# The first 100 microseconds of a decoder layer: zero matmuls ahead of the loads, another order of loads and weights, masks and token shift written later

## The chip, the cores and the metric

The kernel runs on one core of one Trainium2 chip. The metric is the device time of one execution in microseconds; the time before is the median of three executions. A profile is one further execution that the hardware profiler recorded, with a span (first to last instruction) and a time of its own.

## The reference

One hybrid decoder layer over 1024 tokens of width 1024, all in float32:

```python
u = rmsnorm(h, norm1_g)
proj = u @ w_in
p_rwkv, p_att, p_idx, p_gate = jnp.split(proj, c, axis=-1)
y_a = rwkv7_mix(token_shift(p_rwkv, tshift_mu), ...)      # recurrent mixing, 8 heads
q_idx = rope(q_idx.reshape(B, S, IDX_HEADS, IDX_DIM))     # indexer: 8 query heads, one key head
k_idx = rope(k_idx[:, :, None, :])[:, :, 0, :]
y_b = dsa_attention(q, k, v, q_idx, k_idx, w_idx)         # attention over the indexer's top 256 keys
merged = g_a * (y_a @ w_o_rwkv) + g_b * (y_b @ w_o_att)
h = h + merged @ w_out
z_gate, z_up = jnp.split(rmsnorm(h, norm2_g) @ w_ffn_in, 2, axis=-1)
h = h + (jax.nn.silu(z_gate) * z_up) @ w_ffn_out
return rmsnorm(h, normf_g)

def token_shift(p, mu):
    prev = jnp.pad(p, ((0, 0), (1, 0), (0, 0)))[:, :-1]
    return p + (prev - p) * mu
```

## The kernel before

**Arithmetic.** Activations lie with features on the partitions and tokens along the free dimension, in two halves of 512 tokens. To keep float32 accuracy with the fast float32r matmul, every operand is split into a high and a low part (`whi`/`wlo` for weights, `u0hi`/`u0lo` for the first half of x, `u1hi`/`u1lo` for the second). ScalarE makes the high part, VectorE subtracts for the low one, and `mm3` adds up high x high, high x low and low x high: per half 24 matmuls for one 128-column tile of weights and eight tiles of 128 features.

**Opening.** `first` loads two weight tiles (CT_IK, the indexer's key and weights, and CT_WA, the decay and rate columns) and sixteen tiles of x through SP's DMA queue, splits them, and runs both weight tiles over both halves. x is not normalized first: `Rms` sums the squares beside the matmuls (`add`), `columns` and `row` make the reciprocal root, and every result is scaled by it afterwards (`scale`, `rows[half]`).

**Next stage.** `proj_iq` projects the indexer's queries (CT_IQ, CT_IQ + 1), then runs `rest` and the generator `between`, and then projects CT_IQ + 2 and CT_IQ + 3. `rest` applies the token shift (`shifted`, lines 281 to 287) to the CT_WA result, stores it to `d_rw`, rotates the indexer's key (`rope_one`) and stores it to `d_ik`. `between` is the projection of CT_GD with its own token shift. After it come the tiles of k (the first ones before the scores), and `scores` loads `ik` and, for each block of 128 queries, `iq` from DRAM and runs the score matmuls (line 860) with pieces of the remaining projections between them (`pump`).

**What sets the order.** TensorE's instructions stand in the order in which the source writes them:

```python
ctx.enter_context(tc.manual_schedule(engines={mybir.EngineType.PE}))
```

For VectorE, ScalarE, SP's DMA queue and GpSimd a scheduler chooses the order when the kernel is built; each engine and queue then runs its list strictly in order, and waits at the first instruction whose input is not there. Buffers rotate: three accumulators of one PSUM bank each (`acc`), five further banks (`mix`), four temporaries (`tmp`), two staging buffers (`stg`, from which results are stored to DRAM), two pairs of split weights, three raw weight tiles (`wst`). A tile that takes a buffer waits for the last reader of the tile before it; for `stg` that reader is a store.

**Masks.** `masks` loads the causal mask (`caus`) and fills the bias of the first two query blocks at line 836; these biases are read in the attention stage, hundreds of microseconds later.

Of the kernel before, what the change touches and what calls it, by code (L numbers as in the profile page):

```python
# [11 lines left out]
F32 = mybir.dt.float32  # L12
# [37 lines left out]
def block_kernel(ctx: ExitStack, tc: tile.TileContext, ins: dict, outT: bass.AP, stop=None, dbg=None):  # L50
# [54 lines left out]
    def mix():  # L105
        return psM.tile([128, HT], F32, tag="mix", name="mix")
# [10 lines left out]
    def raw_weights(src, nk=8):  # L117
        st = wp.tile([128, nk, 128], F32, tag="wst", name="wst", bufs=3)
        wq[0].dma_start(st, src)
        return st  # L120

    def weights(src, nk=8, rush=True, st=None, pool=None):
        with tc.high_priority() if rush else nullcontext():
            if st is None:
                st = raw_weights(src, nk)
            hi, lo = ((pool or wp).tile([128, nk, 128], F32R, tag=tag, name=tag, bufs=8 if pool else None)
                      for tag in ("whi", "wlo"))
            split(hi, lo, st)
        return hi, lo
# [121 lines left out]
    def gsplit(hi, lo, x, gcol):  # L251

        g = par[:, gcol:gcol + 1]
        A.activation(hi, x, AF.Copy, scale=g)
        V.scalar_tensor_tensor(lo, x, g, hi.bitcast(F32), op0=ALU.mult, op1=ALU.subtract)

    def load_x(half, h, js):
        src = ins["xT"][:, half * HT:(half + 1) * HT].rearrange("(k p) t -> p k t", p=128)
        for j in js:
            SY.dma_start(h[:, j, :], src[:, j, :])  # L260
# [80 lines left out]
    def first(us, xp, pj, cp2, cs):  # L341

        hs = [xp[half].tile([128, 8, HT], F32, tag=f"h{half}", name="h") for half in range(2)]
        st0 = raw_weights(ins["w_in"][CT_IK])
        load_x(0, hs[0], range(2))
        st1 = raw_weights(ins["w_in"][CT_WA])
        load_x(0, hs[0], range(2, 8))
        load_x(1, hs[1], range(8))
        SY.dma_start(cs, ins["rope"])
        ws = [weights(None, st=st, rush=False) for st in (st0, st1)]  # L350
        sqs, raws = [], []
        for half, h in enumerate(hs):
            for k in range(8):
                gsplit(us[half][0][:, k, :], us[half][1][:, k, :], h[:, k, :], P_N1 + k)
            sqs.append(Rms(h))
            for k in range(8):
                sqs[half].add(k)
            uhi, ulo = us[half]
            pss = [acc(), acc()]
            for k in range(8):  # L360
                for (whi, _), ps in zip(ws, pss):
                    T.matmul(ps, whi[:, k, :], uhi[:, k, :], start=k == 0, stop=False)
                    T.matmul(ps, whi[:, k, :], ulo[:, k, :], start=False, stop=False)
            for (_, wlo), ps in zip(ws, pss):
                for k in range(8):
                    T.matmul(ps, wlo[:, k, :], uhi[:, k, :], start=False, stop=k == 7)
            raw = cp2.tile([128, HT], F32, tag=f"raw{half}", name="raw")
            A.activation(raw, pss[0], AF.Copy)
            wa = cp2.tile([128, HT], F32, tag=f"wa{half}", name="wa")
            A.activation(wa, pss[1], AF.Copy)  # L370
            raws.append((raw, wa))
        def scale(half):
            rows[half] = sqs[half].row()
            for i in range(2):
                c = cs[:, i, half * HT:(half + 1) * HT]
                V.tensor_tensor(c, c, rows[half], op=ALU.mult)

        def rest():
            st = stage(pj)
            for half in range(2):  # L380
                shifted(st, half, CT_WA, raws[half][1])
            SY.dma_start(d_rw[CT_WA][0], st.rearrange("p h t -> p (h t)"))
            for half in range(2):
                ik = rope_one(cs, raws[half][0], half)
                kst = stage(pj, F32R)
                split(kst[0:64, 0, :], kst[0:64, 1, :], ik[0:64, :])
                for i in range(2):
                    SY.dma_start(d_ik[half].rearrange("c (p s) t -> s p c t", s=2)[i],
                                 kst[32 * i:32 * i + 32, :, :].bitcast(F32))

        return sqs, scale, rest, raws

    def proj_iq(us, pj, cs, between, sqs, scale, rest, raws):
        off = 256
        sqs[0].columns(rsk[:, 0, :])
        wa = weights(ins["w_in"][CT_IQ], rush=False)
        psa = [mix(), mix()]
        yield from mm3(psa[0][:, :HT - off], wa, us[0], tok=slice(off, HT))
        sqs[1].columns(rsk[:, 1, :])
        yield from mm3(psa[1], wa, us[1])  # L400
        wb = weights(ins["w_in"][CT_IQ + 1])
        for half, o in enumerate((off, 0)):
            ps = acc()
            yield from mm3(ps[:, :HT - o], wb, us[half], tok=slice(o, HT))
            scale(half)
            rope_b(cs, ps, rope_a(cs, psa[half], half, o), pj, [(slice(0, 128), d_iq[half][:, 0:4])], half, o)
        rest()
        yield from between
        yield from proj_rope(CT_IQ + 2, us, pj, cs, lambda half: [(slice(0, 128), d_iq[half][:, 4:8])], off=off)
        for half in range(2):  # L410
            pt = mix()
            for t in range(4):
                T.transpose(pt[:, t * 128:(t + 1) * 128], raws[half][0][:, t * 128:(t + 1) * 128], ident)
            for t in range(4):
                V.tensor_scalar(widx[:, 4 * half + t, :], pt[:, t * 128 + 64:t * 128 + 72], rsk[:, half, t:t + 1],
                                64 ** -0.5 * 8 ** -0.5, op0=ALU.mult, op1=ALU.mult)
            yield 4
# [404 lines left out]
    def masks(bp, p):  # L822

        caus = p.tile([128, 128], F32, name="caus")
        G.dma_start(caus, ins["consts"][:, K_CAUS, :])
        bias, kept = {}, {}
        for b in range(8):
            n = (b + 1) * 128
            if b in LATE:
                kept[b] = bp.tile([128, n], F32, name=f"kept{b}")  # L830
                bias[b] = kept[b].bitcast(BF16)[:, 0:n]
            else:
                bias[b] = bp.tile([128, n], BF16, name=f"bias{b}")
            if b < 2:
                V.memset(bias[b], 0.0)
                V.tensor_scalar(bias[b][:, b * 128:], caus, BIG / 3.0e38, None, op0=ALU.mult)
        bp.tile([128, 16], F32, name="edge")
        return caus, bias, kept

    def scores(keep, p, caus, kept):  # L840

        ik = p.tile([128, 2, S], F32R, name="ik")
        for h in range(2):
            for e in range(2):
                SY.dma_start(ik[64 * e:64 * e + 64, :, h * HT:(h + 1) * HT].bitcast(F32),
                             d_ik[h].rearrange("c p t -> p c t"))
        sc = {}
        for b in range(2, 8):
            n = (b + 1) * 128
            iq = p.tile([128, 8, 128], F32R, tag="iq", name="iq", bufs=2)  # L850
            o = (b % 4) * 128
            for i in range(2):
                SY.dma_start(iq[64 * i:64 * i + 64, :, :].bitcast(F32),
                             d_iq[b // 4][i, :, :, o:o + 128].rearrange("h p t -> p h t"))
            s = kept[b] if b in kept else keep.tile([128, n], F32, tag=f"sc{b}", name="sc")
            for c, w in pieces(n):
                for h in range(8):
                    ps = mix()
                    for i in range(2):
                        T.matmul(ps[:, :w], iq[:, h, :], ik[:, i, c:c + w], start=i == 0, stop=i == 1)  # L860
                    rl = p.tile([128, 512], F32, tag="rl", name="rl", bufs=3)
                    A.activation(rl[:, :w], ps[:, :w], AF.Relu)
                    if h == 0:
                        V.tensor_scalar(s[:, c:c + w], rl[:, :w], widx[:, b, 0:1], 0.0, op0=ALU.mult, op1=ALU.add)
                    else:
                        V.scalar_tensor_tensor(s[:, c:c + w], rl[:, :w], widx[:, b, h:h + 1], s[:, c:c + w],
                                               op0=ALU.mult, op1=ALU.add)
                    pump(2)
            V.tensor_tensor(s[:, n - 128:n], s[:, n - 128:n], caus, op=ALU.add)
            sc[b] = s  # L870
        return sc
# [544 lines left out]
```

## Time and profile before

| | |
|---|---|
| median of three executions | 1773.98 us (1772.75 to 1774.41) |
| profiled execution, its own time | 1776.56 us |
| its span | 1774.8 us |
| mean granted TensorE clock | 0.993 |
| TensorE busy | 1731.5 us |
| VectorE busy | 1117.6 us |
| ScalarE busy | 832.2 us |

In the lines of the profile, PE is TensorE's matmuls, PEld its weight loads, DVE VectorE, ACT ScalarE, POOL GpSimd, and SPq the DMA queue that SyncE issues. A line of a timeline has the start, the time taken, the engine, the line of the source, the operation, the tile written and the tiles read, the shapes and how many instructions were merged; in brackets stands how long the engine had been idle and what ended the idling. A line of waits has who waited for whom, the sum in microseconds, how often, and the longest. Matmuls are pipelined, so the time of one is longer than the step from its start to the next one's.

### The profile page before, as it was taken

The numbers are of one execution on the slowest core, as the hardware profiler recorded it, in microseconds if no ns is written. First come the engines' busy times: TensorE is split into PE (matmuls) and PEld (weight loads), VectorE is DVE, ScalarE is ACT, GpSimd is POOL, SyncE is SP. The second block draws the span as 40 slices with busy tenths as digits, with TensorE's granted clock in tenths as the row PEclk, the third lists the DMA queues.
The fourth block names the chain that finished last, engine by engine and source line by source line (L and its number), as shares of the span: only waits on it lengthen the run. The fifth ranks groups of instructions, "written<-read, shape, count | busy, mean of one in ns | idle before, by whom it ended". The sixth has DMA issues, their size and how long they took to land. (4 is left out here: it accounts for less than half of the span.)

```text
span 1774.8 us, 26838 instructions
## 1 busy us (share of the span) xinstructions
PE 1731.5 (98%) x10256; PEld 1432.1 (81%) x10256; DVE 1117.6 (63%) x2137; ACT 832.2 (47%) x1535; POOL 93.5 (5%) x120
## 2 busy tenths in 40 slices
PE   7999999999999999999999999999999999999997
PEld 6888888788888777777888888888788888888877
DVE  5779989866468568847865655524565564454464
ACT  6355998453444788654233455523334322232231
POOL 0000000010021110001000311000000000000000
PEclk9999999999999999999999999999999999999999
DMA  5542224536375535723244854243565344434441
GB/s 207 165 138 90 101 95 143 164 86 176 92 203 171 148 108 173 227 88 110 78 119 113 240 154 119 76 139 112 185 206 154 108 135 148 143 97 156 129 139 64
DMA packets 130992, 244.00 MB, mean 137 GB/s; under 512 B 36536, under 2 KB 59704, under 8 KB 130736
## 3 DMA queue, kind: packets, MB, share of 16 engines
q1 hardware_dynamic: 107472, 168.38, 30.7%
q10 hardware_dynamic: 15552, 47.75, 8.8%
q0 software_dynamic: 7840, 26.15, 5.6%
q8 instruction: 81, 1.33, 0.3%
q14 instruction: 47, 0.39, 0.1%
HBM read 189.29 MB, written 52.95 MB: 136 GB/s over the span
## 5 line engine op out<-in xcount | busy, mean ns | idle before, releaser
L113 DVE TENSOR_TENSOR wlo<-wst,whi 128x1024 fp32r<-128x1024 f32 (+1 forms) x231 | 277.8, 1204 | 306.1 <-PE acc L143 139.7
L112 ACT ACTIVATE whi<-wst 128x1024 fp32r<-128x1024 f32 (+1 forms) x231 | 240.6, 1043 | 282.3 <-PE acc L139 224.0
L138 PE MATMUL acc<-zhi,whi 128*128 128x512 f32 x672 | 265.8, 396 | 1.3 <-DVE tmp L1189 1.3
L139 PE MATMUL acc<-zlo,whi 128*128 128x512 f32 x672 | 262.8, 391 | 0.0
L143 PE MATMUL acc<-zhi,wlo 128*128 128x512 f32 x672 | 170.1, 392 | 0.0
L138 PEld LDWEIGHTS acc<-zhi,whi 128*128 128x128 f32 x672 | 126.8, 189 | 28.5 <-issue 3.4
L138 PE MATMUL acc<-fhi,whi 128*128 128x512 f32 (+1 forms) x400 | 145.0, 371 | 3.9 <-ACT fhi L112 3.9
L139 PEld LDWEIGHTS acc<-zlo,whi 128*128 128x128 f32 x672 | 126.8, 189 | 25.0
L143 PEld LDWEIGHTS acc<-zhi,wlo 128*128 128x128 f32 x672 | 124.8, 188 | 25.5 <-issue 0.7
L139 PE MATMUL acc<-flo,whi 128*128 128x512 f32 (+1 forms) x400 | 143.7, 367 | 1.4 <-DVE flo L113 1.2
L138 PE MATMUL acc<-u1hi,whi 128*128 128x512 f32 x352 | 140.5, 399 | 0.1
L138 PE MATMUL acc<-u0hi,whi 128*128 128x512 f32 (+1 forms) x352 | 135.3, 387 | 4.2 <-DVE tmp L281 2.4
L139 PE MATMUL acc<-u1lo,whi 128*128 128x512 f32 x352 | 137.6, 391 | 0.0
L139 PE MATMUL acc<-u0lo,whi 128*128 128x512 f32 (+1 forms) x352 | 133.7, 382 | 0.0
L143 PE MATMUL acc<-fhi,wlo 128*128 128x512 f32 (+1 forms) x400 | 92.6, 369 | 0.0
L138 PEld LDWEIGHTS acc<-fhi,whi 128*128 128x128 f32 x400 | 76.1, 190 | 17.9 <-ACT fhi L112 5.8
L143 PE MATMUL acc<-u1hi,wlo 128*128 128x512 f32 x352 | 89.7, 394 | 0.0
L139 PEld LDWEIGHTS acc<-flo,whi 128*128 128x128 f32 x400 | 76.2, 190 | 14.6 <-DVE flo L113 3.3
L143 PE MATMUL acc<-u0hi,wlo 128*128 128x512 f32 (+1 forms) x352 | 86.0, 384 | 0.0
L112 ACT ACTIVATE fhi<-tmp 128x512 fp32r<-128x512 f32 x44 | 27.8, 631 | 113.7 <-DVE tmp L1169 113.7
L138 PEld LDWEIGHTS acc<-u0hi,whi 128*128 128x128 f32 x352 | 66.1, 188 | 17.5 <-issue 2.6
L143 PEld LDWEIGHTS acc<-fhi,wlo 128*128 128x128 f32 x400 | 69.6, 191 | 12.1 <-issue 0.5
(304 smaller groups left out, 3146.0 us busy)
## 6 DMA issues: line engine op xcount, KB each, us to landing
wst<-in_w_ffn_in SPq DMA_DIRECT2D x72, 512.0 KB, 3.7
wst<-in_w_in ACTq DMA_DIRECT2D x36, 512.0 KB, 3.7
wst<-in_w_in SPq DMA_DIRECT2D x27, 512.0 KB, 3.7
wst<-in_w_fo SPq DMA_DIRECT2D x25, 512.0 KB, 3.7
k<-d_k POOLq DMA_DIRECT2D x24, 512.0 KB, 8.3
h<-in_xT SPq DMA_DIRECT2D x32, 256.0 KB, 5.2
d_g<-tmp ACTq DMA_DIRECT2D x32, 256.0 KB, 3.0
tmp<-d_g SPq DMA_DIRECT2D x32, 256.0 KB, 3.1
```

The lines of the kernel that those rows point to most:

```text
L112: A.activation(hi, x, AF.Copy)
L113: V.tensor_tensor(lo, x, hi.bitcast(F32), op=ALU.subtract)
L138: T.matmul(ps, whi[:, wk + k, :], ahi[:, ak + k, tok], start=k == 0, stop=False)
L139: T.matmul(ps, whi[:, wk + k, :], alo[:, ak + k, tok], start=False, stop=False)
L143: T.matmul(ps, wlo[:, wk + k, :], ahi[:, ak + k, tok], start=False, stop=k == nk - 1)
```

## The change

Four edits, all of the first stage.

- Six float32 matmuls over the zeroed state tile are written ahead of everything else on TensorE; nothing reads their results.
- The loads of x come three tiles, then the second weight tile, then the rest (before: two, weight, rest). The weights' high parts are written where the loads arrive, their low parts after all eight low parts of the first half of x. On TensorE the first weight tile runs three feature tiles ahead of the second.
- In `proj_iq` the projection of CT_GD (`between`) comes before `rest`.
- The multiplies that fill the first two biases move from `masks` to the start of `scores`.

```diff
     def first(us, xp, pj, cp2, cs):
         hs = [xp[half].tile([128, 8, HT], F32, tag=f"h{half}", name="h") for half in range(2)]
+        for _ in range(6):
+            T.matmul(mix()[:, 0:256], state[:, 0:2, :].rearrange("p c t -> p (c t)"),
+                     state.rearrange("p c t -> p (c t)"), start=True, stop=True)
+        lead = 3
         st0 = raw_weights(ins["w_in"][CT_IK])
-        load_x(0, hs[0], range(2))
+        load_x(0, hs[0], range(lead))
         st1 = raw_weights(ins["w_in"][CT_WA])
-        load_x(0, hs[0], range(2, 8))
+        load_x(0, hs[0], range(lead, 8))
         load_x(1, hs[1], range(8))
         SY.dma_start(cs, ins["rope"])
-        ws = [weights(None, st=st, rush=False) for st in (st0, st1)]
+        ws = [tuple(wp.tile([128, 8, 128], F32R, tag=tag, name=tag) for tag in ("whi", "wlo")) for _ in range(2)]
         sqs, raws = [], []
         for half, h in enumerate(hs):
+            if half == 0:
+                A.activation(ws[0][0], st0, AF.Copy)
             for k in range(8):
+                if half == 0 and k == lead:
+                    A.activation(ws[1][0], st1, AF.Copy)
                 gsplit(us[half][0][:, k, :], us[half][1][:, k, :], h[:, k, :], P_N1 + k)
+            if half == 0:
+                for (whi, wlo), st in zip(ws, (st0, st1)):
+                    V.tensor_tensor(wlo, st, whi.bitcast(F32), op=ALU.subtract)
             ...
-            for k in range(8):
-                for (whi, _), ps in zip(ws, pss):
-                    T.matmul(ps, whi[:, k, :], uhi[:, k, :], start=k == 0, stop=False)
-                    T.matmul(ps, whi[:, k, :], ulo[:, k, :], start=False, stop=False)
+            for i in range(8 + lead):
+                for (whi, _), ps, k in zip(ws, pss, (i, i - lead)):
+                    if 0 <= k < 8:
+                        T.matmul(ps, whi[:, k, :], uhi[:, k, :], start=k == 0, stop=False)
+                        T.matmul(ps, whi[:, k, :], ulo[:, k, :], start=False, stop=False)
     ...
     def proj_iq(us, pj, cs, between, sqs, scale, rest, raws):
+        yield from between
         rest()
-        yield from between
     ...
     def masks(bp, p):
                 V.memset(bias[b], 0.0)
-                V.tensor_scalar(bias[b][:, b * 128:], caus, BIG / 3.0e38, None, op0=ALU.mult)
     ...
     def scores(keep, p, caus, kept):
+        for b in range(2):
+            V.tensor_scalar(bias[b][:, b * 128:], caus, BIG / 3.0e38, None, op0=ALU.mult)
         ik = p.tile([128, 2, S], F32R, name="ik")
```

## The prediction

> **What bounds the kernel now.** I read the page first, then the waits of TensorE, then the timeline of the first 100 us engine by engine, because the change touches nothing later.
>
> ```profile
> span 1774.8 us, 26838 instructions
> ...
> PE 1731.5 (98%) x10256; PEld 1432.1 (81%) x10256; DVE 1117.6 (63%) x2137; ACT 832.2 (47%) x1535; POOL 93.5 (5%) x120
> ```
>
> TensorE is busy for 98% of the span, and its instructions stand in a fixed order. A delay that TensorE gets early therefore stays until the end, and a wait that goes is a gain, unless another wait opens behind it. The answer on TensorE's waits in the first 200 us has three rows:
>
> ```profile
> PE acc L362 <- ACT u0hi L254: 6.7, 1, 6.7
> PE acc L363 <- DVE u0lo L255: 2.7, 1, 2.7
> PE acc L138 <- DVE tmp L281: 2.4, 1, 2.4
> ```
>
> Two belong to the opening (nothing loaded, then no low part of x), and the third is an accumulator that VectorE had not emptied. These 11.8 us are all that the change can win by waits. Because the rest is one queue of matmuls, I walk the changed kernel's built instruction order with the durations below until TensorE meets its first wait-free stretch; in that order 13 instructions of ScalarE, 26 of VectorE and 9 of SP's queue stand elsewhere than before, all of them in the first 110 us.
>
> **Opening: masks and low parts.** The timeline of VectorE:
>
> ```profile
> 8.00 0.36 DVE L836 TENSOR_SCALAR bias<-caus 128x128 bf16<-128x128 f32 x2 [2.86 <-DMA caus<-in_consts]
> 8.28 1.22 DVE L113 TENSOR_TENSOR wlo<-wst,whi 128x1024 fp32r<-128x1024 f32 x1
> 9.42 1.41 DVE L255 SCALAR_TENSOR_TENSOR u0lo<-h,par,u0hi 128x512 fp32r<-128x512 f32 x2
> 10.74 1.22 DVE L113 TENSOR_TENSOR wlo<-wst,whi 128x1024 fp32r<-128x1024 f32 x1
> ```
>
> The first low part of x ends near 10.1, behind the two mask multiplies (which wait for their load until 8.00) and a weight's low part of 1.22. The source of the changed kernel writes the multiplies and the weights' low parts later, but a scheduler orders VectorE, and the built order still has both mask multiplies first, then the first `wlo`, then three `u0lo` (two before), the second `wlo`, and the other five. So the first low part is as late as before, and these edits bring nothing: that part of the change doesn't do what it says. The fourth low part now ends near 13.3: 9.42 + 3 x 0.67 = 11.4, the `wlo` to 12.6, one more `u0lo`. The second weight's load moves back by one x tile of 0.26 MB, 0.65 us at the 401 GB/s that the first window further down shows; its low part ran at 10.74 before and is wanted at 11.4 now, so nothing waits.
>
> **Opening: matmuls on zeros.** The timeline of TensorE:
>
> ```profile
> 6.72 0.79 PE L362 MATMUL acc<-u0hi,whi 128*128 128x512 f32 x1 [6.72 <-ACT u0hi L254]
> 10.22 0.79 PE L363 MATMUL acc<-u0lo,whi 128*128 128x512 f32 x1 [2.70 <-DVE u0lo L255]
> ...
> 13.79 0.63 PE L363 MATMUL acc<-u0lo,whi 128*128 128x512 f32 x1
> 14.22 0.52 PE L362 MATMUL acc<-u0hi,whi 128*128 128x512 f32 x1
> 14.58 0.40 PE L363 MATMUL acc<-u0lo,whi 128*128 128x512 f32 x1
> 14.81 0.39 PE L362 MATMUL acc<-u0hi,whi 128*128 128x512 f32 x1
> ```
>
> and, from the same view much later, the nearest float32 matmul of this size:
>
> ```profile
> 381.83 1.89 PE L622 MATMUL mix<-x,blk 128*128 128x256 f32 x8
> ```
>
> Until 14.5 a matmul starts every 0.43 us, then every 0.23: the clock is half at first (the page prints 1.00 there for want of a record). The change issues six float32 matmuls of 256 columns once the state tile is cleared, near 1.4. L622 has eight records, two to a matmul, in 1.89 (the last one's 0.38 overlaps the next line's work), so about 0.45 each at full clock and 0.9 at half: 5.4 us, to 6.8. They cost nothing themselves, because TensorE has nothing else until 6.72 and the next matmul needs the low part at 10.2; the PSUM buffers that they write are not wanted before the second half of x is through. After them TensorE has one matmul and then 3 us of idling. Does the clock survive that? The windows before and after two clock records:
>
> ```profile
> 11.08:14.49 3.41, 3.41 (x9) 2.64 (x9) 3.41 (x5) 3.41 (x7) 0.00 (x0) 1.00 1.05 401
> 843.93:847.30 3.37, 3.18 (x14) 2.96 (x15) 2.89 (x7) 0.24 (x1) 0.00 (x0) 0.50 0.55 158
> 847.30:850.76 3.46, 3.46 (x11) 2.78 (x10) 3.46 (x6) 2.13 (x4) 0.00 (x0) 0.50 0.02 5
> 1277.40:1280.84 3.44, 1.92 (x7) 0.86 (x5) 2.22 (x5) 2.77 (x5) 0.00 (x0) 1.00 0.80 291
> 1280.84:1284.25 3.41, 3.38 (x8) 2.71 (x9) 1.17 (x2) 1.06 (x1) 0.00 (x0) 0.50 0.54 156
> ```
>
> Columns: length, busy time of TensorE, weight loads, VectorE, ScalarE and GpSimd, then the granted clock. A window in which TensorE was busy for 1.92 of 3.44 is followed by one at half clock; a window busy for 3.18 of 3.37 did not bring the full clock back; one busy throughout (11.08 to 14.49) did. Three idle microseconds cannot be cut by a window's edge so that both sides keep more than 56%. So I take the clock as half again at 10.2. Then the new order of the first weight ahead of the second hurts: before the fourth low part (13.3) it offers only seven matmuls, the last at 12.52, so TensorE idles for about 0.4 and is one matmul behind at 14.5 (10 issued, not 11): +0.2. If the idle moment also denies that window the full clock, as 3.18 of 3.37 was denied, the next 3.4 us hold 8 matmuls instead of 15: +1.8 in all. I take +1.8, nearest to that row; the ends are +0.2 and, with the clock full from 10.2, 41 matmuls of 0.227 from 13.3 to 22.6, against 37 from 14.58 to 23.0: -0.4.
>
> [...]
>
> **Token shift later.** VectorE's timeline, then TensorE's:
>
> ```profile
> 65.32 1.22 DVE L113 TENSOR_TENSOR wlo<-wst,whi 128x1024 fp32r<-128x1024 f32 x1 [1.07 <-PE acc L143]
> ...
> 69.72 0.68 DVE L281 TENSOR_TENSOR tmp<-acc,row 128x512 f32<-128x512 f32 x1
> ```
>
> ```profile
> 66.98 1.12 PE L143 MATMUL acc<-u0hi,wlo 128*128 128x256 f32 x8
> 70.55 0.35 PE L138 MATMUL acc<-u0hi,whi 128*128 128x256 f32 x1 [2.45 <-DVE tmp L281]
> ```
>
> In the new order the first accumulator of the tile CT_GD is read at 59.8, ahead of the token shift: the 2.45 us go. What is late next: the shift, the halo and the key rotation, which filled VectorE's idling before 65.32, now stand behind that `wlo` and ahead of the two reads that free the next accumulator. From 65.32: `wlo` 1.15, four shifts of 0.67, three products and seven rotation steps of 0.6, two half reads of 0.34, small ones 0.35: 10.9, to 76.2. TensorE asks for it after 24 matmuls of 0.12 and 24 of 0.227 from 67.9, at 76.3. That is level. One step, at 74.6, needs a ScalarE copy of 0.6 into a staging buffer whose store to DRAM goes out at 69.7; with the 3.3 to 5.9 us of landing shown below that copy ends at 73.6 to 76.2, so the wait is 0 to 1.6, and I take 0.3, since a store that lands in 4.6 adds 0.3.
>
> **What it puts into SP's queue.** This is the expensive part. SP's queue, the landing time of the `iq` loads, the first score matmul, and VectorE around it:
>
> ```profile
> 87.00 0.57 SPq L853 DMA_DIRECT2D iq<-d_iq  x1
> 89.16 0.98 SPq L315 DMA_DIRECT2D d_iq<-stg  x2
> 90.18 2.88 SPq L853 DMA_DIRECT2D iq<-d_iq  x3
> 97.72 0.35 SPq L119 DMA_DIRECT2D wst<-in_w_in  x1
> 100.05 0.34 SPq L294 DMA_DIRECT2D d_rw<-stg  x1
> ```
>
> ```profile
> DMA to landing us min/median/max: 3.3/5.2/5.9
> ```
>
> ```profile
> 99.83 0.51 PE L860 MATMUL mix<-ik,iq 128*128 128x384 f32 x2
> ```
>
> ```profile
> 96.47 1.23 DVE L113 TENSOR_TENSOR wlo<-wst,whi 128x1024 fp32r<-128x1024 f32 x1 [1.73 <-PE acc L143]
> 97.61 0.68 DVE L281 TENSOR_TENSOR tmp<-acc,row 128x512 f32<-128x512 f32 x1
> 99.09 0.75 DVE L283 SCALAR_TENSOR_TENSOR stg<-tmp,par,stg 128x511 f32<-128x511 f32 x1 [0.79 <-ACT stg L282]
> 99.76 0.21 DVE L287 SCALAR_TENSOR_TENSOR stg<-halo,par,stg 128x1 f32<-128x1 f32 x1
> ```
>
> The first score matmul (L860, 99.83) needs both halves of the first `iq` tile; before, they are issued at 87.00 and 90.18. In the changed order SP's queue holds, one behind the other: the `d_ik` stores, two weights that wait for VectorE's `wlo`, the `d_iq` stores and `ik` loads, one more weight (the one of 97.72), the first half of `iq`, the store `d_rw` of the first k tile (the one of 100.05), and only then the second half of `iq`. SP waits in order, so this half cannot be issued before that store, which hangs on the chain of 96.47 to 99.76 behind TensorE's own last matmul of that tile. The store comes at 100.05 less what TensorE has gained by then; the load is issued 0.38 later, and lands 3.3 to 5.9 later (all loads of this tile between 60 and 130 us). TensorE stands at the first score matmul, which it would reach 0.22 before the store: a wait of L + 0.6, with L the landing. I take L = 4.6, the middle, since two 512 KB transfers go just ahead: a wait of 5.2.
>
> Such a wait costs more than itself: at least one window is mostly idle, so the matmuls behind it run at half clock for one window (3.4 us, loss 1.7, as at 1280.84) or two (3.4, as from 843.93). I take 1.7.
>
> **Sum.** Gain before the scores: 2.45 - 0.3 - 1.8 = 0.35. Then 0.6 + 4.6 - 0.35 = 4.85 late at the first score, and 1.7 for the clock: +6.5. The profiled execution took 1776.56 (1774.8 of span and 1.8 around it), so 1783.1 by its own measure; carried to the median of 1773.98, 1780.5. Ends: +3.4 (opening +0.2, no wait after the shift, L 3.3, one half window) to +10.9 (+1.8, 1.6, 5.9, two windows): 1777.4 to 1784.9. Two high tiles of the second half that ScalarE now makes before it empties an accumulator are at nothing, since TensorE reads them after 23. Behind the first score matmul the built order is the old one, and TensorE has no wait there before 200 us in which the delay could vanish.
>
> **Rivals.**
> 1. The load is in time, and the kernel is faster. The second half of `iq` would have to land before TensorE's arrival near 97 to 99, so be issued before about 94. Then only the gain stays: -0.4 (0.35) to -2.9 (opening -0.4, no wait), and about -4.5 if unprofiled runs pay a half window after the old 2.45 us wait. For it: before, the loads landed with over 2 us to spare. Against: the store ahead in the queue, whose data does not exist by then. Chance 0.12; 1770 to 1773.6, likeliest 1772.
> 2. The clock stays full through both gaps: opening -0.4, a gain of 2.85, then 0.6 + L - 2.85 with L 3.3 to 4.6 and no half window: +1.1 to +2.4, 1775 to 1776.4. For it: the dummies do keep TensorE busy for 5.4 us, more than a window. Against: the row at 1277.40. Chance 0.14. [...]
> 3. Later than my upper end: the wait after the shift takes 1.6, the load 5.9 and the clock more than two windows; above 1784.9. Chance 0.04.
>
> **How the numbers follow.** The forecast has 0.70 and its own range of 1777.4 to 1784.9. Rival 2 and most of the forecast are held by 1775.5 to 1784.5, with rival 1 and the tail left out. A measurement of this kernel can tell 0.2%, 3.5 us, from no change. Faster by more needs the far end of rival 1: 0.04. Within it lie rival 2, the rest of rival 1 and the low edge of the forecast: 0.14 + 0.08 + 0.03 = 0.25. Slower by more: 0.71.
>
> **What would show it.** Right: both mask multiplies still ahead of the first `wlo` at about 8 us; a TensorE wait of some 0.4 on the fourth `u0lo`; no wait on L281 near 70; the `iq` load behind the `d_rw` store at about 100; one wait of 4 to 6.5 us on the first score matmul, released by a DMA, and a half-clock record behind it. Wrong: matmuls 0.23 apart from 10.2 on, or a first score matmul before 99.8.

## Result and the profile after

The changed kernel takes 1781.83 us (median of 13 executions, 1778.01 to 1786.71) beside 1774.41 us for the kernel before: ratio 1.0031, interval 1.0017 to 1.0045. (The two medians alone stand 0.42% apart; the ratio is the estimate that comes with the interval.) In a second comparison it was 1.0020 (1.0009 to 1.0032). The change makes the kernel 0.20 to 0.31% slower, some 3.6 to 5.5 us. The profiled execution has a span of 1780.3 us and 1782.03 us as its own time.

The first lines of the page of the changed kernel:

```profile
span 1780.3 us, 26872 instructions
...
PE 1738.2 (98%) x10268; PEld 1437.0 (81%) x10268; DVE 1117.8 (63%) x2137; ACT 831.9 (47%) x1535; POOL 93.4 (5%) x120
```

TensorE's waits in the first 200 us:

```profile
PE mix L873 <- DMA iq<-d_iq: 5.9, 1, 5.9
PE acc L375 <- DVE u0lo L255: 2.5, 2, 2.3
PE mix L345 <- DVE S L479: 1.2, 1, 1.2
PE acc L138 <- DVE tmp L301: 0.6, 1, 0.6
PE acc L374 <- ACT u0hi L254: 0.3, 1, 0.3
```

The wait of 2.4 on L281 is gone, and a wait of 5.9 on a load of `iq` has come. The opening's 6.7 is only filled: the matmuls on zeros run in it, and the first matmul on x still starts at 6.85. TensorE's timeline, opening to first score (line 873 is 860 of before):

```profile
1.23 5.32 PE L345 MATMUL mix<-S 128*128 128x256 f32 x12 [1.23 <-DVE S L479]
6.85 0.50 PE L374 MATMUL acc<-u0hi,whi 128*128 128x512 f32 x1 [0.31 <-ACT u0hi L254]
9.61 0.78 PE L375 MATMUL acc<-u0lo,whi 128*128 128x512 f32 x1 [2.25 <-DVE u0lo L255]
...
12.73 0.64 PE L375 MATMUL acc<-u0lo,whi 128*128 128x512 f32 x1 [0.21 <-DVE u0lo L255]
...
22.32 0.39 PE L374 MATMUL acc<-u1hi,whi 128*128 128x512 f32 x1
...
76.41 0.50 PE L138 MATMUL acc<-u1hi,whi 128*128 128x512 f32 x1 [0.62 <-DVE tmp L301]
...
103.53 0.98 PE L873 MATMUL mix<-ik,iq 128*128 128x384 f32 x2 [5.93 <-DMA iq<-d_iq]
```

VectorE, with the masks where they were, and SP's queue ahead of the first score:

```profile
7.40 0.36 DVE L854 TENSOR_SCALAR bias<-caus 128x128 bf16<-128x128 f32 x2 [2.25 <-DMA caus<-in_consts]
7.68 1.22 DVE L365 TENSOR_TENSOR wlo<-wst,whi 128x1024 fp32r<-128x1024 f32 x1
8.81 2.07 DVE L255 SCALAR_TENSOR_TENSOR u0lo<-h,par,u0hi 128x512 fp32r<-128x512 f32 x3
10.80 1.22 DVE L365 TENSOR_TENSOR wlo<-wst,whi 128x1024 fp32r<-128x1024 f32 x1
```

```profile
96.31 0.57 SPq L866 DMA_DIRECT2D iq<-d_iq  x1
98.14 0.34 SPq L294 DMA_DIRECT2D d_rw<-stg  x1
98.53 2.26 SPq L866 DMA_DIRECT2D iq<-d_iq  x3
```

The second half of the first `iq` tile is the first of the three loads at 98.53, behind the `d_rw` store; it lands at 103.40, and the matmul that needs it starts 0.13 later. Before, the two halves went out at 87.00 and 90.18. The clock, in windows (length, busy time of TensorE, weight loads, VectorE, ScalarE, GpSimd, then the granted clock):

```profile
6.25:9.66 3.41, 0.85 (x4) 0.24 (x2) 2.26 (x5) 2.36 (x4) 0.00 (x0) 1.00 1.00 371
9.66:13.07 3.41, 3.20 (x7) 2.05 (x8) 3.41 (x5) 3.41 (x6) 0.00 (x0) 0.50 1.05 404
13.07:16.48 3.41, 3.41 (x16) 2.78 (x16) 3.31 (x6) 3.41 (x7) 0.00 (x0) 1.00 1.05 406
98.41:101.82 3.41, 0.00 (x0) 0.00 (x0) 0.00 (x0) 0.00 (x0) 0.00 (x0) 1.00 1.07 341
101.82:105.23 3.41, 1.70 (x5) 1.53 (x6) 0.16 (x1) 0.49 (x1) 0.00 (x0) 0.50 0.91 183
105.23:108.64 3.41, 3.41 (x11) 2.93 (x10) 1.38 (x3) 0.98 (x2) 0.00 (x0) 0.50 0.00 0
108.64:112.05 3.41, 3.41 (x18) 3.05 (x17) 2.54 (x6) 2.36 (x5) 0.00 (x0) 1.00 0.01 2
```

With the zeros the first clock record, 1.00, comes at 6.25; the clock is at 0.50 from 9.66 to 13.07, and at 0.50 for two more windows (101.82 to 108.64) behind the 5.93 us wait on `iq`.

Since TensorE's order is nearly the same in both kernels, the start of each of its matmuls after, less its start before, shows where time goes. This delay is -0.66 us from 23 to 67 us, -3.32 behind the vanished wait on L281, -2.38 behind the wait on L301, +3.71 at the first scores, +6.12 behind the half clock, and it ends at +5.46.

### The profile page after: what moved, and what is told of

Its sections match the earlier page's. It is cut to its first block, busy times and chain, and to the rows that moved or that the text cites. A ratio compares the mean times of both kernels' runs of the same rounds, so it can differ in the third digit from the quotient of the medians.

```text
span 1780.3 us, 26872 instructions
## 1 busy us (share of the span) xinstructions
PE 1738.2 (98%) x10268; PEld 1437.0 (81%) x10268; DVE 1117.8 (63%) x2137; ACT 831.9 (47%) x1535; POOL 93.4 (5%) x120
```

## The experiments

The delay in the table is this difference to the profile of before, taken between 110 and 130 us; u1 is the start of the first matmul on the second half of x (22.98 before).

| kernel | ratio to before, interval | u1, us | delay at 110 to 130 us |
|---|---|---|---|
| changed | 1.0031 (1.0017 to 1.0045) | 22.32 | +6.12 |
| changed, second time (j_after) | 1.0020 (1.0009 to 1.0032) | 22.73 | +6.34 |
| before, as a variant (i_before) | 1.0010 (0.9995 to 1.0025) | 22.24 | -0.75 |
| changed, order of the shift undone (a_unswap) | 0.9989 (0.9975 to 1.0003) | 23.37 | +0.40 |
| before, order of the shift alone (b_swap) | 1.0022 (1.0007 to 1.0036) | 23.40 | +5.74 |
| changed, first `iq` tile on GpSimd's queue (c_iqpool) | 0.9989 (0.9974 to 1.0003) | 24.60 | +1.72 |
| changed, masks on GpSimd (d_maskpool) | 1.0018 (1.0008 to 1.0028) | 24.52 | +7.72 |
| changed without zeros (h_nozeros) | 1780.55 us, one execution | 23.28 | +5.45 |
| before with 6 zeros (e_zeros6) | 1769.83 us, one execution | 22.56 | -0.42 |
| before with 13 zeros (e_zeros13, k_zeros13) | 0.9973 (0.9959 to 0.9986), 0.9978 (0.9964 to 0.9992) | 21.35, 21.33 | -1.64, -0.37 |
| changed, shift undone, 13 zeros (l_unswap13) | 0.9977 (0.9964 to 0.9989) | 22.64 | +0.95 |
| changed, 13 zeros, two `iq` tiles on GpSimd's queue (f_best) | 0.9969 (0.9954 to 0.9984) | 22.53 | +1.04 |

**What the comparison resolves.** The kernel before against itself:

> The kernel before itself, unchanged, timed as if it were a variant: what the comparison makes of no change at all. Theory (the comparison is even): ratio within 0.9985 to 1.0015, second half of x between 22.9 and 23.5 us. Rival (a kernel in this place reads 2 to 3 us less, which would explain why the two unswapped variants and the zeros read that much below what their profiles account for): ratio 0.998 to 0.9985.

It read 1.0010. Executions of one kernel differ by several microseconds, and their granted clock differs with them: of the executions of before in this comparison the fastest took 1768.70 us at a mean clock of 0.996, the slowest 1782.67 at 0.990. The half-clock windows do not fall in the same places: between 690 and 870 us the profile of before has four of them, that of `i_before` five. The opening differs too: `i_before` reaches the second half of x 0.74 us earlier (22.24 for 22.98, where 22.9 to 23.5 was expected), with no edit at all. Differences of 0.1% are therefore not read from times here, only from traces.

**The order of the token shift.** Undone in the changed kernel, and made alone in the kernel before:

```diff
 # a_unswap (after), b_swap (before) the other way round
-        yield from between
         rest()
+        yield from between
```

> The changed kernel with one part undone: the token shift (`between`) is emitted ahead of `rest()` again; zeros, weight order, order of the low parts and late masks stay. Theory (the 5.93 us wait for the second half of the first `iq` tile is all the loss, and it comes from the order of SP's queue, which this part sets): the wait on `iq` is gone, the 2.45 us wait at L281 is back, first score near 99.83 - 0.66 = 99.2 us, time 0.7 us under the kernel before, near 1773.7 us, ratio 0.9996. Rival (the opening's rush and its clock cost the 6 us): `iq` wait gone too, but the time stays near 1780, ratio over 1.002.

> The kernel before with that one part alone: `rest()` ahead of `between`. Theory: the whole loss without any of the opening: wait at L281 (2.45 us) gone, a wait of 0 to 0.6 us at L301, a wait of 5.9 us on the first `iq` tile at L873, then some 5 us or more at half clock (2.5 us lost): -2.45 + 0.3 + 5.9 + 2.5 = +6.2 us, near 1780.6 us, ratio 1.0035. Rival (the stall comes of the shifted start after the opening, not of the order): no wait over 1 us at L873, and the time 2 us under the kernel before, ratio 0.999.

In `a_unswap` the wait on `iq` is gone, SP issues its halves at 87.40 and 90.59, and the wait on L281 is back. Its first score starts at 100.23, not at 99.2 as expected, because its opening ran 1.05 us longer than in the changed kernel; its ratio is 0.9989 for 0.9996, which lies inside the interval. In `b_swap` the whole stall is there without any of the opening's edits. TensorE's waits in the first 200 us of each:

```profile
PE acc L375 <- DVE u0lo L255: 3.3, 2, 3.1
PE acc L138 <- DVE tmp L281: 2.4, 1, 2.4
PE mix L345 <- DVE S L479: 1.2, 1, 1.2
PE acc L374 <- ACT u0hi L254: 1.0, 1, 1.0
```

```profile
PE acc L362 <- ACT u0hi L254: 6.7, 1, 6.7
PE mix L860 <- DMA iq<-d_iq: 5.7, 1, 5.7
PE acc L363 <- DVE u0lo L255: 2.3, 1, 2.3
```

and the queue of `b_swap`:

```profile
96.51 0.57 SPq L853 DMA_DIRECT2D iq<-d_iq  x1
98.33 0.34 SPq L294 DMA_DIRECT2D d_rw<-stg  x1
98.73 2.26 SPq L853 DMA_DIRECT2D iq<-d_iq  x3
```

This one line of the source makes the loss. The time of `b_swap` is lower than expected (1.0022 for 1.0035), with the expectation inside the interval.

**Is it the queue?** The first tile's loads on another queue:

```diff
-                SY.dma_start(iq[64 * i:64 * i + 64, :, :].bitcast(F32),
+                (G if b == 2 else SY).dma_start(iq[64 * i:64 * i + 64, :, :].bitcast(F32),
```

> The changed kernel with one edit: the two loads of the first `iq` tile (block 2) are issued on GpSimd's queue in place of SP's, so that neither stands behind the store of the first k tile. Theory (the load is late only because SP issues it after that store): first score at about 103.53 - 5.93 = 97.6 us, no half clock after it, and the time 5.93 + 2.5 = 8.4 us less than the changed kernel, 2 to 3 us less than the kernel before, near 1772 us, ratio 0.9985. Rival 1 (the transfer itself is what takes the time, behind other traffic): the wait at L873 keeps 2 us or more. Rival 2 (GpSimd's queue holds the load back, or its own work waits behind it): the wait moves to another tile and the time stays within 2 us of the changed kernel.

GpSimd issues both loads at 93.13 to 94.58, and the 5.9 us wait and its half clock are gone:

```profile
78.77 0.50 PE L138 MATMUL acc<-u1hi,whi 128*128 128x512 f32 x1 [0.70 <-DVE tmp L301]
...
100.00 0.58 PE L873 MATMUL mix<-ik,iq 128*128 128x384 f32 x2
...
108.00 0.70 PE L873 MATMUL mix<-ik,iq 128*128 128x512 f32 x2 [1.29 <-DMA iq<-d_iq]
```

So the place in SP's queue made the wait. On GpSimd's queue the second of the two loads lands at 99.91, only just in time. And the 2.45 us of L281 are not kept either. The delay goes from +1.62 in the opening to -1.05 where that wait was, and is +1.72 by 110 us: 0.70 us of waiting at L301, a step of 0.45 in place of 0.23 ahead of the first score, and 1.29 on the next `iq` tile, whose second half still follows the store. Without its stall the swap gains nothing in this trace. The expected 0.9985 was too good; 0.9989 cannot be told from it.

**The masks.** The multiplies off VectorE:

```diff
-            V.tensor_scalar(bias[b][:, b * 128:], caus, BIG / 3.0e38, None, op0=ALU.mult)
+            G.tensor_scalar(bias[b][:, b * 128:], caus, BIG / 3.0e38, None, op0=ALU.mult)
```

> The changed kernel with the two mask multiplies on GpSimd: VectorE's first `wlo` no longer stands behind the 2.25 us wait for `caus`. Theory (that wait alone holds the first low part at 9.61 us, and opened the gap in which the clock fell at 9.66): `wlo` starts near 5.7 us, the first matmul with a low part at 7.5 to 8.0 us, no half clock at 9.66; but the second weight tile and x still land at the same times, so that the second half of x starts 0 to 1.5 us earlier than 22.32 and the time stays within 1.5 us of the changed kernel, near 1781, ratio 1.003 to the kernel before. Rival (the masks are no bound): first low part still after 9 us.

TensorE's timeline, VectorE's second `wlo`, and the windows:

```profile
6.71 0.50 PE L374 MATMUL acc<-u0hi,whi 128*128 128x512 f32 x1 [1.26 <-ACT u0hi L254]
7.74 0.50 PE L375 MATMUL acc<-u0lo,whi 128*128 128x512 f32 x1 [0.53 <-DVE u0lo L255]
...
11.47 0.80 PE L374 MATMUL acc<-u0hi,whi 128*128 128x512 f32 x1 [0.91 <-ACT u0hi L254]
12.78 0.79 PE L375 MATMUL acc<-u0lo,whi 128*128 128x512 f32 x1 [0.51 <-DVE u0lo L255]
```

```profile
10.84 1.23 DVE L365 TENSOR_TENSOR wlo<-wst,whi 128x1024 fp32r<-128x1024 f32 x1 [0.82 <-ACT whi L361]
```

```profile
7.45:10.86 3.41, 2.22 (x5) 0.86 (x5) 1.75 (x4) 2.02 (x4) 1.25 (x2) 1.00 1.04 404
10.86:14.28 3.42, 2.29 (x5) 1.50 (x6) 3.42 (x5) 3.42 (x6) 0.00 (x0) 0.50 1.05 404
14.28:17.69 3.41, 3.41 (x10) 2.64 (x9) 3.10 (x6) 3.41 (x8) 0.00 (x0) 0.50 1.09 427
```

The masks did hold up the first low part: its matmul now starts at 7.74, not 9.61. But nothing of this head start is left at the fourth low part, whose matmul starts at 12.78 (12.73 in the changed kernel): it stands behind the second `wlo`, and that one starts at 10.84 (10.80), now because it waits for ScalarE's high part of the second weight. The clock was expected to stay full, and did not: a window busy for 2.22 of 3.41 us is followed by two at half clock, until 17.69, just when there is work enough for it. The second half of x starts 2.2 us later than in the changed kernel, where I had expected it no later. That delay is not shown to be the masks' doing: `c_iqpool`, with the masks where they were, had half-clock windows from 11.08 to 17.9 and started the second half at 24.60. The ratio, 1.0018, is below the 1.003 expected, and is close to what the changed kernel itself gave the second time. Starting early gained nothing here.

**The zeros.** In the kernel before alone (13, then 6), and left out of the changed kernel:

```diff
+        for _ in range(13):        # e_zeros13; 6 in e_zeros6; none in h_nozeros
+            T.matmul(mix()[:, 0:256], state[:, 0:2, :].rearrange("p c t -> p (c t)"),
+                     state.rearrange("p c t -> p (c t)"), start=True, stop=True)
```

> The kernel before with 13 zeros matmuls ahead of the opening and nothing else. Theory (the clock is lost again in the opening because TensorE idles between the zeros and the first low part; with zeros enough to reach from 1.2 to about 9 us it stays): full clock from 4 to 6.3 us on without a break up to 100 us; the second half of x starts 0.5 to 1.3 us ahead of the 22.98 of before, no wait on `iq`; time 1 us less, ratio 0.9990 to 1.0000. Rival (the clock falls anyway, or the zeros hold up real work): the second half of x at 23 us or later.

> The kernel before with the change's 6 zeros matmuls and nothing else. Theory: full clock from 4 to 6.3 us, lost again between 7.5 and 11 us, back one or two windows of 3.41 us later; so the second half of x starts anywhere from 22.2 to 24.7 us (22.98 before), by where the windows fall against the idle gap; the rest as before. Rival (six zeros are enough to keep the clock): no record of half clock before 100 us.

> The changed kernel without its zeros matmuls. Theory: the first record of full clock comes at 13 to 16 us, as in the kernel before (14.49), and none at half clock follows it before 98 us; the second half of x starts at 22.9 to 23.6 us; the wait on the first `iq` tile stays at 5.5 to 6 us and the half clock after it too, time 1780 to 1784 us. Rival (the zeros and the clock that they lose are part of the loss): the second half of x ahead of 22.3 us.

With 13 the matmuls on zeros last until the first low part is there:

```profile
1.23 8.11 PE L345 MATMUL mix<-S 128*128 128x256 f32 x26 [1.23 <-DVE S L470]
...
9.92 0.50 PE L366 MATMUL acc<-u0lo,whi 128*128 128x512 f32 x1 [0.34 <-DVE u0lo L255]
...
12.38 0.50 PE L366 MATMUL acc<-u0lo,whi 128*128 128x512 f32 x1 [0.35 <-DVE u0lo L255]
...
21.35 0.39 PE L365 MATMUL acc<-u1hi,whi 128*128 128x512 f32 x1
```

From 5.79 to 1261 us no window is at half clock. The opening gains 1.62 us on the profile of before and 0.89 on that of `i_before`; 0.5 to 1.3 was expected. The ratio, 0.9973, is below the expected 0.9990 to 1.0000. With 6 the clock falls at 11.26 for one window, and the second half of x starts at 22.56, between the two profiles without zeros (22.24 and 22.98): six show no gain. Without zeros the changed kernel has its first record of full clock at 14.78, no half clock until 100.11, and the same stall (6.0 us). The zeros are not part of the loss.

**Once more, and together.** The changed kernel again, the 13 zeros again, and both with the shift's order undone:

> The changed kernel once more, in the company of the kernels below. Theory: ratio 1.0025 to 1.0040 as in the first comparison (1.0031), a wait of 5.5 to 6.0 us on the first `iq` tile, full clock from 4 to 7.5 us, lost again in the opening, and the second half of x anywhere from 22.2 to 24.7 us. Rival (what the two kernels that kept the late load showed, 1.0018 and 1.0022, is the change's true price): ratio 1.0015 to 1.0023.

> The kernel before with 13 zeros matmuls, once more. Its opening gained 1.62 us, its time 4.8 us (ratio 0.9973). Theory (the opening's clock is all that the zeros bring, the rest was chance in where the later half-clock windows fell): ratio 0.9985 to 1.0000, the second half of x at 21.3 to 21.8 us. Rival (the zeros bring more, by fewer half-clock windows at 740 to 860 us): ratio 0.9965 to 0.9980 again, and fewer than four such windows there.

> The changed kernel with the token shift put back ahead of `rest()` and 13 zeros matmuls in place of 6: it differs from the kernel before with 13 zeros only in the order of the first loads, weights and low parts, and in the late masks. Theory (that order costs about 1.1 us: with the clock full, the second half of x started at 22.53 us with it and at 21.35 us without): the second half of x at 22.3 to 22.7 us, no wait on `iq`, ratio 0.9990 to 1.0003, about 1 us more than the kernel before with 13 zeros. Rival (the order is free, and the 1.1 us came from where the loads landed in that run): the second half of x at 21.3 to 21.8 us.

The changed kernel's second ratio, 1.0020, missed the expected 1.0025 to 1.0040 and lies in the rival's 1.0015 to 1.0023, as do `b_swap` (1.0022) and `d_maskpool` (1.0018), which kept the late load; so the price of the change is likelier near 0.2% than 0.3%, though the intervals overlap. Its trace shows the same stall (5.7 us) and the same two half-clock windows.

`k_zeros13` differs from `l_unswap13` in the order of the first loads, weights and low parts and in the masks alone, and both keep the full clock in the opening: 21.33 against 22.64 us. `e_zeros13` (21.35) and `f_best` below (22.53) show the same pair. With the clock full, the new order of the opening costs 1.2 to 1.3 us; in `l_unswap13` the fourth low part is awaited for 1.07 us at 13.19, behind the second `wlo`. In the times this cost does not show: `l_unswap13` was expected at 0.9990 to 1.0003 and gave 0.9977, no more than `k_zeros13`. The 13 zeros repeat their ratio (0.9978): the rival, that they bring more than the opening, holds, but not by its reason, for `k_zeros13` has four half-clock windows between 690 and 870 us, as many as before. What they bring besides shows at 760 us. TensorE's timeline there in the kernel before, then with 6 zeros:

```profile
758.89 1.07 PE L721 MATMUL mix<-TT,TZ 32*32 32x32 f32 x55
760.44 0.34 PE L721 MATMUL mix<-TT,TZ 32*32 32x32 f32 x9 [0.48 <-issue]
```

```profile
758.56 1.20 PE L724 MATMUL mix<-TT,TZ 32*32 32x32 f32 x64
```

In all four traces without zeros TensorE pauses after 55 or 56 of these 64 small matmuls, for 0.48 to 1.05 us, with no releaser, and a half-clock window follows (from 762.01 in the profile of before); in all ten with zeros it does not. In those the delay falls by 2.2 us at this place (in the changed kernel from +7.99 to +5.77). The zeros put 6 or 13 more matmuls in front and shift the rotation of the `mix` buffers. No run separates the two, and none shows what makes the pause.

Last, the change's gains without its stall:

```diff
-        for _ in range(6):
+        for _ in range(13):
     ...
-                SY.dma_start(iq[64 * i:64 * i + 64, :, :].bitcast(F32),
+                (G if b < 4 else SY).dma_start(iq[64 * i:64 * i + 64, :, :].bitcast(F32),
```

> The changed kernel with 13 zeros matmuls in place of 6, and with all four loads of the first two `iq` tiles (blocks 2 and 3) on GpSimd's queue. Theory (this keeps the change's two gains and drops its loss): full clock from 6.3 us on, second half of x at 22.0 to 22.4 us, first score at 97 to 98 us with no wait at L873 over 0.5 us and no half clock behind it; time 0.9 + 2.45 - 0.7 = 2.6 us under the kernel before, ratio 0.9985. Rival 1 (four loads in a row on GpSimd's queue land later than two): a wait of 1 us or more at L873, time within 1 us of the kernel before. Rival 2 (the opening's clock falls all the same): the second half of x after 23 us and time within 1 us of the kernel before.

The first score starts at 99.25 after a wait of 2.24 us for which the profile names no releaser, but the second load of its tile, issued at 90.98, landed at 99.15; the four loads on GpSimd's queue, issued from 90.22 on, took 9.2 us to land (median), against 5.0 for two of them in `c_iqpool`. That is the first rival, and one half-clock window follows. The delay of +1.04 at 110 us less the 2.2 at 760 makes 0.9993, and its 0.9969 is better than that; its trace has no half clock between 850 and 1761 us, which no edit explains, so I do not count it as better than the 13 zeros alone. The kernel before with 13 zeros is the only one that was faster than the kernel before in two comparisons, by 0.2 to 0.3%.

## Why the prediction was right, and where not

The forecast of 1780.5 us and its side were right, and the main mechanism was the one named: the store of the first k tile stands ahead of the second half of `iq` in SP's queue. But the first and the last term were too high and three between them too low, so part of the agreement is luck. The measured column is one pair of profiles, and `i_before`, with no edit, differs from the same profile of before by -0.74 in the opening and +2.15 at the end.

| step | predicted, us | measured, us |
|---|---|---|
| opening | +1.8 | -0.66 |
| wait on L281 goes | -2.45 | -2.66 |
| wait behind the shift | +0.3 | +0.94 (0.62 of it the wait) |
| wait at the first score | +5.2 | +6.09 (5.93 of it the wait) |
| half clock behind it | +1.7 | +2.41 |
| after 110 us | 0 | -0.66 |
| sum | +6.5 | +5.46 |

- **Masks and low parts.** Right: both multiplies stay ahead of the first `wlo`, and the fourth low part is awaited (0.21 us, 0.4 forecast). They ran 0.6 us earlier because the wait for `caus` ended earlier.
- **Zeros and the clock.** Right that the clock would be lost between zeros and first low part (busy 0.85 of 3.41 us, then 0.50). The step that failed is the last one, which took 3.18 of 3.37 as proof that an idle moment denies the full clock: 3.20 of 3.41 was followed by it (and in `k_zeros13`, in the last section, 2.96). With the same built order up to there, the second half started at 22.32, 22.73, 23.37 and 24.60 us in four traces, in the order in which their half-clock windows ended (13.07, 13.62, 14.72 and 17.9); the fourth low part came within 0.6 us in all of them (12.73 to 13.30). The +1.8 is one end of what happens (+1.62 in `c_iqpool`), not its middle, and the measured -0.66 is no gain of the change, since `i_before` has -0.74. Rival 2, with the clock full through both gaps, failed at both (0.50 from 9.66 and from 101.82). The busy share alone did not tell what followed: after 2.22 of 3.41 us the clock was half in `d_maskpool` (from 10.86), after 1.97 of 3.41 it was full in the kernel before (from 72.52, last section).
- **Token shift.** Right: the wait on L281 goes, and the new one, 0.62, lies in the 0 to 1.6 given.
- **SP's queue.** Right, with two terms of the wait too small: the load landed 4.87 us after its issue (4.6 taken) and the matmul started 0.13 later, and TensorE stood there 0.54 us before the store went out (0.22 taken). Rival 1 failed by its own condition: the load was issued at 98.5, not before 94.
- **Clock behind the stall.** The mechanism was right, the size was not: two windows, not one, in each of the five traces with that stall. They cost 2.41 us here, not the 3.4 given for two, for the first of them was busy for 1.70 us only.
- **Nothing after 110 us.** Wrong: 2.2 us came back at 760 us, in every trace with zeros and in none without, while other half-clock windows fell differently. I had no row for it, because I costed the zeros only where they run.

## What to carry to other kernels

Of a step that is moved on the compute engines, read the built order of every DMA queue as well: here an emission order worth 2.45 us on VectorE put a load behind a store whose data did not yet exist, and cost 5.9 us and two half-clock windows. A wait that is removed can come back in pieces behind it, as in `c_iqpool` (0.70 us at L301, 1.29 on the next `iq` tile); so see what is late next, here for some 40 us on. Filler matmuls paid here where they reached up to the first steady work: six left a gap of 3.03 us and showed no gain (second half of x at 22.56, without zeros at 22.24 and 22.98), thirteen left 0.34 (21.35). And compare with a second profile of the unchanged kernel before calling a microsecond a gain.

## What the runs showed of the hardware

The wait at L281, 2.4 us in both, was followed by half clock in `k_zeros13` and not in the kernel before. Windows around it in `k_zeros13`, then in the kernel before:

```profile
65.03:68.44 3.41, 1.42 (x12) 1.22 (x11) 3.41 (x7) 1.01 (x2) 0.00 (x0) 1.00 0.67 228
68.44:71.86 3.42, 2.96 (x14) 3.00 (x15) 2.66 (x7) 1.43 (x3) 0.61 (x1) 0.50 0.49 161
```

```profile
69.11:72.52 3.41, 1.97 (x16) 2.00 (x17) 2.95 (x8) 0.63 (x1) 0.55 (x1) 1.00 0.82 270
```

In the first a window busy for 1.42 us is followed by half clock, and the delay grows by 1.3 us; in the second TensorE was busy for 1.97 us and the clock stayed. The same wait had two prices; what decides between them was not tested.

The pause without releaser among the small matmuls at 760 us is 0.48 us in the profile of before, 0.96 in `i_before`, 0.8 in `b_swap` and 1.05 in `h_nozeros`; the ten traces with zeros show none there. No edit was aimed at it, so its cause is not shown.
